# Hybrid SSD/GLA trunk, output stage: the norm's row scaling issued later, another arithmetic for the last two row pairs, and the last product in two halves

## The chip, the core and the metric

One NeuronCore of a Trainium2 chip runs the whole program as one launch. The metric is the device time of that launch in microseconds (us); each kernel is run several times and the median counts. Engines are called as in the profile: PE is the matrix engine (PEld its weight load), DVE the vector engine, ACT the scalar engine, POOL the GpSimd engine, SP the engine that here only issues DMAs. Each engine works through its own queue in order; a DMA is issued by an engine's queue and then moves by itself, and an instruction or a DMA issue whose data or buffer is not ready holds up what is behind it in that queue.

## The reference, cut to what matters

The kernel computes one layer of a decoder trunk on 2048 tokens of width 1024, in float32. `u = rmsnorm(h)` goes through one input projection into two branches (a Mamba-2 SSD scan and a gated linear attention), both are projected, gated and added to `merged`, and the end of it is

```python
merged = jnp.sum(gates * branch_proj, axis=2)
h = hres + jnp.einsum('bld,de->ble', merged, w_out)
...
out = rmsnorm(h, final_norm_w)[:, N_META:]   # x * rsqrt(mean(x*x) + EPS) * w, row by row
```

The change touches only this last product with `w_out`, the residual sum and the final row norm.

## The kernel before, in words

The kernel first runs the input projections and the two scans over four blocks of 512 tokens, and then seven stages of 1024-wide products (gates and two branch projections for each half of the tokens, then the output stage). Only the output stage, the last of the seven, is touched.

**Products.** Every stage multiplies 2x2 blocks by seven products in place of eight (a Strassen-like scheme). A float32 operand is split into a rounded high part and the rest (`hl`), so one block product of 128 rows, depth 512 and 512 columns is four depth steps of three matmuls (`accum`, L187 to L191): 12 matmuls of 128x128 by 128x512. In the output stage a "pair" is two tiles of 128 rows (i = 0 and 1) by two column halves (t = 0 and 1); there are 8 pairs, worked in four groups of two, and within a group the products run in the order `PS = (1, 2, 6, 7, 5, 3, 4)`, each for both pairs of the group: 14 products in a group, 56 in the stage. In the last group products 4 and 3 change places (L1112 to L1118).

**Banks and snapshots.** For a pair, products 1, 6, 5 and 3 add up in one PSUM bank ("a", printed as `pj`), 7 and 4 in another ("b", `pt`), 2 in a third ("c", `pc`). After products 1, 6 and 5 ACT copies bank "a" into an SBUF tile `sn` (`snapshot`, L1007, its instruction is L1010), and the next product into bank "a" waits for that copy. A quarter of the output is complete after products 2, 5, 4 and 3 (`DONE`, L1013); each then is handed to the stage's `use`: products 2 and 5 complete the first, 3 and 4 the second quarter of a row tile. `total` (L1023, its DVE add is L1026) adds bank and snapshot.

**Output stage** (`out_stage`, L1068). `fetch` loads a quarter of the residual x into a tile `io` (L1074, issued by SP; 8 such buffers, so exactly one group's quarters). `use` (L1080) adds the product to it on DVE (L1084: `r = 0.5*x + r`), squares it on ACT with a row sum into `ssf` (L1090), and when both quarters of a row tile are there: two tiny DVE instructions make mean + EPS (L1092, L1093), POOL raises it to -0.5 (L1094), and DVE scales both quarters by that column and by the norm weights (L1097, two instructions). `store` (L1016) only notes the two quarters; `flush` (L1162) issues the notes as DMAs from the ACT queue (L1164) after the next product, and what is left at the end of the program goes out from SP (L1215).

**What sets the order.** `at(position, fn)` books work at a product's position, and the main loop (L1206 to L1215) traces product, flush, booked work. `prep_a` (L980) splits a left operand on ACT (L983) and DVE (L984) five products ahead; `load_a` and `sum_a` (L962, L971) load the next group's left operands into tiles `ar` and form their sums `as` on POOL (L974 to L977), nine products ahead. SP's queue is exactly in traced order (`manual_schedule`). For all other engines, PE among them, a list scheduler at build time orders the instructions by its own estimate of when each can start; traced order is a priority there. Waits between engines follow from the tiles.

## Time and profile before

| what | value |
|---|---|
| device time, median of 3 runs | 2293.7 us (2292.3 to 2297.49) |
| device time of the profiled execution | 2293.83 us |
| its span, first to last instruction | 2292.0 us |
| mean granted PE clock | 0.994 |
| PE busy | 2232.7 us, 97% of the span |
| DVE, ACT, POOL busy | 68%, 51%, 30% |
| output stage's share | its matmuls run from about 2120 us to 2280.6 us of the span |

In a timeline row the columns are the start and the duration in us, engine and line, operation, output<-inputs, shapes, count; in square brackets how long the engine had been idle before and what ended that. "q" behind an engine means its queue, for DMA issues. In a row of the windows view they are the stretch, its length, then for PE, PEld, DVE, ACT and POOL the busy us with the number of instructions, the granted PE clock, the busy share of the DMA engines and GB/s. In the waits view a row is: who waited, for whom, us in total, times, longest.

### The profile page before, as it was taken

The numbers are of one execution on the slowest core, as the hardware profiler recorded it, in microseconds if no ns is written. First come the engines' busy times: TensorE is split into PE (matmuls) and PEld (weight loads), VectorE is DVE, ScalarE is ACT, GpSimd is POOL, SyncE is SP. The second block draws the span as 40 slices with busy tenths as digits, with TensorE's granted clock in tenths as the row PEclk, the third lists the DMA queues.
The fourth block names the chain that finished last, engine by engine and source line by source line (L and its number), as shares of the span: only waits on it lengthen the run. The fifth ranks groups of instructions, "written<-read, shape, count | busy, mean of one in ns | idle before, by whom it ended". The sixth has DMA issues, their size and how long they took to land. (4 is left out here: it accounts for less than half of the span.)

```text
span 2292.0 us, 36448 instructions
## 1 busy us (share of the span) xinstructions
PE 2232.7 (97%) x12641; PEld 1944.7 (85%) x12641; DVE 1549.2 (68%) x2895; ACT 1180.1 (51%) x2726; POOL 683.8 (30%) x681
## 2 busy tenths in 40 slices
PE   7899999999999999999999999899999999999997
PEld 6899989888889988888888898778888888788776
DVE  5677676675666676667667666674678845788766
ACT  4665655465534455544455544454544545454443
POOL 3344433122222122211212100066333274323331
PEclk9999999999999999999999999999999999999999
DMA  8766776667787676877667654466768865787743
GB/s 298 234 208 216 272 258 211 219 205 231 245 270 218 221 225 208 264 256 245 206 220 223 219 185 157 130 216 211 234 224 292 300 226 197 245 278 262 244 145 121
DMA packets 301544, 518.04 MB, mean 226 GB/s; under 512 B 27696, under 2 KB 143664, under 8 KB 301360
## 3 DMA queue, kind: packets, MB, share of 16 engines
q1 hardware_dynamic: 200400, 402.84, 54.4%
q10 hardware_dynamic: 100960, 112.88, 14.2%
q8 instruction: 99, 1.62, 0.3%
q14 instruction: 85, 0.70, 0.1%
HBM read 368.42 MB, written 147.19 MB: 225 GB/s over the span
## 5 line engine op out<-in xcount | busy, mean ns | idle before, releaser
L189 PE MATMUL pj<-ue,whl 128*128 128x264 f32 (+1 forms) x672 | 238.8, 355 | 12.3 <-ACT acc L492 6.3
L191 PE MATMUL pj<-ue,whl 128*128 128x264 f32 (+1 forms) x672 | 232.3, 346 | 0.6 <-DVE tkc L399 0.6
L190 PE MATMUL pj<-ue,whl 128*128 128x264 f32 (+1 forms) x672 | 231.3, 344 | 0.0
L189 PE MATMUL pj<-uo,whl 128*128 128x512 f32 x512 | 206.6, 404 | 0.0
L191 PE MATMUL pj<-uo,whl 128*128 128x512 f32 x512 | 200.1, 391 | 0.0
L190 PE MATMUL pj<-uo,whl 128*128 128x512 f32 x512 | 199.4, 389 | 0.0
L82 POOL TENSOR_TENSOR wr<-wr 128x256 f32<-128x256 f32 x80 | 68.5, 857 | 430.6 <-DMA wr<-u 176.2
L189 PE MATMUL pj<-b,a 128*128 128x512 f32 x480 | 189.4, 396 | 6.6 <-ACT sn L1010 5.8
L191 PE MATMUL pj<-b,a 128*128 128x512 f32 x480 | 188.6, 393 | 0.0
L190 PE MATMUL pj<-b,a 128*128 128x512 f32 x480 | 187.8, 391 | 0.7 <-DVE b L959 0.7
L170 POOL TENSOR_TENSOR whl<-wr,whl 128x512 fp32r<-128x512 f32 (+1 forms) x100 | 134.0, 1347 | 181.0 <-ACT whl L169 132.8
L974 POOL TENSOR_TENSOR as<-ar,ar 128x512 f32<-128x512 f32 x40 | 59.1, 1476 | 396.3 <-DMA ar<-in_w_br 114.2
L496 DVE SCALAR_TENSOR_TENSOR acc<-cin,hcw,acc 128x512 f32<-128x512 f32 (+1 forms) x192 | 154.6, 805 | 28.8 <-ACT acc L492 27.9
L984 DVE TENSOR_TENSOR a<-ar,a 128x512 fp32r<-128x512 f32 x160 | 125.5, 793 | 57.0 <-ACT a L983 55.3
L959 DVE TENSOR_TENSOR b<-br,b 128x512 fp32r<-128x512 f32 x140 | 120.5, 877 | 52.6 <-ACT b L958 50.7
L189 PEld LDWEIGHTS pj<-ue,whl 128*128 128x128 f32 x672 | 128.9, 192 | 29.9 <-ACT acc L492 7.4
L189 PE MATMUL pj<-whl,ue 128*128 128x256 f32 (+1 forms) x496 | 144.1, 291 | 2.1 <-ACT ue L315 2.1
L189 PE MATMUL pj<-whl,uo 128*128 128x256 f32 (+1 forms) x496 | 143.3, 289 | 0.6 <-DMA whl<-k_zm 0.6
L191 PEld LDWEIGHTS pj<-ue,whl 128*128 128x128 f32 x672 | 128.9, 192 | 15.8 <-POOL whl L170 0.9
L191 PE MATMUL pj<-whl,ue 128*128 128x256 f32 (+1 forms) x496 | 140.6, 284 | 1.4 <-DVE ue L317 1.4
L190 PEld LDWEIGHTS pj<-ue,whl 128*128 128x128 f32 x672 | 129.1, 192 | 14.8
L191 PE MATMUL pj<-whl,uo 128*128 128x256 f32 (+1 forms) x496 | 140.8, 284 | 0.0
(308 smaller groups left out, 6535.2 us busy)
## 6 DMA issues: line engine op xcount, KB each, us to landing
whl<-k_s SPq DMA_DIRECT2D x96, 512.0 KB, 4.3
whl<-k_g SPq DMA_DIRECT2D x96, 512.0 KB, 4.2
whl<-k_v SPq DMA_DIRECT2D x48, 512.0 KB, 3.8
whl<-k_z SPq DMA_DIRECT2D x36, 512.0 KB, 3.7
wr<-in_w_feat SPq DMA_DIRECT2D x64, 256.0 KB, 4.4
k_s<-whl SPq DMA_DIRECT2D x32, 512.0 KB, 3.7
cb<-cumd ACTq DMA_DIRECT2D x64, 256.0 KB, 5.7
y<-gg ACTq DMA_DIRECT2D x64, 256.0 KB, 4.4
```

The source lines that it names most:

```text
L82: nc.gpsimd.tensor_tensor(o, x, y, op=ALU.subtract)
L170: nc.gpsimd.tensor_tensor(hl[:, 1], raw, hl[:, 0].bitcast(F32), op=ALU.subtract)
L189: nc.tensor.matmul(ps, sh, mh, start=first, stop=False, **kw)
L190: nc.tensor.matmul(ps, sh, ml, start=False, stop=False, **kw)
L191: nc.tensor.matmul(ps, sl, mh, start=False, stop=last, **kw)
L496: nc.vector.scalar_tensor_tensor(acc, cin[:, k:k + tt], hcw[:, ti, k:k + 1], acc, op0=ALU.mult, op1=ALU.add)
L959: nc.vector.tensor_tensor(t[:, 1], raw, t[:, 0].bitcast(F32), op=ALU.subtract)
L974: nc.gpsimd.tensor_tensor(s1, a21, a22, op=ALU.add)
L984: nc.vector.tensor_tensor(t[:, 1], src, t[:, 0].bitcast(F32), op=ALU.subtract)
```

## The change

1. **Row scaling later.** For the 12 row tiles whose last product is not among the last four of the stage, the mean and the power (`scale`) are traced one product after the row's last product, and the two scalings with their stores (`finish`) three products after it. `tc.issue_after` queues their DVE instructions behind the DVE instruction traced last (`latest`: an operand split or a residual add); it orders the queue and adds no wait.
2. **Last two pairs** (the last group): the snapshot is added to the residual first (`r += 0.5*snap`, SBUF only), then the bank (`r += 0.5*bank`), in place of bank into snapshot and the sum into r. As many DVE instructions as before; the bank is read by the second of them.
3. **PE order.** In the last 14 products PE too keeps traced order.
4. **The last product** is traced as two halves of 256 columns, 12 matmuls each, in one bank, each half with its own residual add and square. Its `ssf` tile has a third column.
5. **Last four rows' scaling** (`at_once`): not delayed. Three quarters that complete early in the last group are multiplied by the norm weights as soon as their squares are taken; in the last three rows ACT then scales the early quarter by the row factor (`AF.Identity` with a scale column) while DVE scales the late one. In the very last row the norm weights are multiplied in before the factor is known, the second half's multiplication queued behind the last mean instruction.

The diff, shortened:

```diff
@@ prep_a
-            nc.vector.tensor_tensor(t[:, 1], src, t[:, 0].bitcast(F32), op=ALU.subtract)
+            latest[:] = [nc.vector.tensor_tensor(t[:, 1], src, t[:, 0].bitcast(F32), op=ALU.subtract)]
@@ product
+            if (self, n, p) == order[-1]:
+                for c in (slice(0, HB), slice(HB, BLK)):
+                    for j in range(4):
+                        bt = self.b[p, j]
+                        accum(ps[:, c], (a[:, 0, j], a[:, 1, j]), (bt[:, 0, c], bt[:, 1, c]), False, j == 3,
+                              skip_group_check=True)
+                    self.use(n, *DONE[p], ps, None, c)
+                return
@@ out_stage
-        def use(n, i, t, ps, snap):
-            r0 = (2 * n + i) * P
+        def use(n, i, t, ps, snap, cols=None):
             r = res[n, i, t]
-            x = total(ps, snap)
-            nc.vector.scalar_tensor_tensor(r, x, 0.5, r, op0=ALU.mult, op1=ALU.add)
+            if snap is not None and n >= seq // (2 * P) - 2:
+                nc.vector.scalar_tensor_tensor(r, snap, 0.5, r, op0=ALU.mult, op1=ALU.add)
+            else:
+                ps = total(ps, snap)
             first = (n, i) not in ssq
             if first:
-                ssq[n, i] = mk(spl, [P, 2], F32, "ssf")
+                ssq[n, i] = mk(spl, [P, 3], F32, "ssf", bufs=8)
             q = ssq[n, i]
             jk = mk(spl, [P, BLK], BF16, "junk", bufs=1)
-            nc.scalar.activation(jk, r, AF.Square, accum_out=q[:, t:t + 1])
-            if not first:
-                nc.vector.tensor_tensor(q[:, 0:1], q[:, 0:1], q[:, 1:2], op=ALU.add)
-                nc.vector.tensor_scalar(q[:, 0:1], q[:, 0:1], 1.0 / D, EPS, op0=ALU.mult, op1=ALU.add)
-                nc.gpsimd.tensor_tensor(q[:, 0:1], q[:, 0:1], mhalf[:, 0:1], op=ALU.pow)
-                for hf in range(2):
-                    o = res[n, i, hf]
-                    nc.vector.scalar_tensor_tensor(o, o, q[:, 0:1], fns[hf], op0=ALU.mult, op1=ALU.mult)
-                    store(out[r0:r0 + P, hf * BLK:(hf + 1) * BLK], o)
+            c = cols or slice(0, BLK)
+            k = t + (c.start > 0)
+            latest[:] = [nc.vector.scalar_tensor_tensor(r[:, c], ps[:, c], 0.5, r[:, c], op0=ALU.mult, op1=ALU.add)]
+            nc.scalar.activation(jk[:, c], r[:, c], AF.Square, accum_out=q[:, k:k + 1])
+            row = n, i, t
+            if row == at_once[-1] or (first and (n, i) in [w[:2] for w in at_once[1:]]):
+                if k < 2:
+                    nc.vector.tensor_tensor(r[:, c], r[:, c], fns[t][:, c], op=ALU.mult)
+                if k == 1 and not first:
+                    mean(q)
+                if k == 2:
+                    last = nc.vector.scalar_tensor_tensor(q[:, 0:1], q[:, 2:3], 1.0 / D, q[:, 0:1],
+                                                          op0=ALU.mult, op1=ALU.add)
+                    nc.gpsimd.tensor_tensor(q[:, 0:1], q[:, 0:1], mhalf[:, 0:1], op=ALU.pow)
+                    with tc.issue_after(last.ins):
+                        nc.vector.tensor_tensor(r[:, c], r[:, c], fns[t][:, c], op=ALU.mult)
+                    finish(*row)
+            elif row in at_once:
+                scale(*row)
+                finish(*row)
...
+        def finish(n, i, t):
...
+            if (n, i, t) in at_once[1:]:
+                nc.scalar.activation(early, early, AF.Identity, scale=q)
+                if (n, i, t) == at_once[-1]:
+                    nc.vector.tensor_scalar(late, late, q, None, op0=ALU.mult)
+                else:
+                    nc.vector.scalar_tensor_tensor(late, late, q, fns[t], op0=ALU.mult, op1=ALU.mult)
+            else:
+                for o, fn in ((early, fns[1 - t]), (late, fns[t])):
+                    nc.vector.scalar_tensor_tensor(o, o, q, fn, op0=ALU.mult, op1=ALU.mult)
+            for hf, o in ((1 - t, early), (t, late)):
+                store(out[r0:r0 + P, hf * BLK:(hf + 1) * BLK], o)
+
+        def behind(fn, *row):
+            with tc.issue_after(latest[0].ins):
+                fn(*row)
+
+        for i, (n, p) in enumerate(out_order):
+            row = n, *DONE.get(p, (0, 0))
+            if p in (3, 4) and i + 4 < len(out_order):
+                later.append((i + 1, lambda row=row: behind(scale, *row)))
+                later.append((i + 3, lambda row=row: behind(finish, *row)))
+            elif p in (3, 4):
+                at_once.append(row)
@@ main loop
+        if i == len(order) - 2 * len(PS):
+            run_out.close()
+            run_out.enter_context(tc.manual_schedule(engines={mybir.EngineType.PE, mybir.EngineType.SP}))
```

`scale` is `mean` and the POOL power, `mean` the two tiny DVE instructions.

More of the change, by code (lines that the diff above doesn't have):

```diff
@@ L1011, in snapshot @@
             self.snap[n, p] = sn
+    latest, later, order = [], [], []
     DONE = {2: (0, 0), 5: (1, 1), 4: (1, 0), 3: (0, 1)}
@@ new lines, in mean, with scale @@
+        def mean(q):
+            nc.vector.tensor_tensor(q[:, 0:1], q[:, 0:1], q[:, 1:2], op=ALU.add)
+            nc.vector.tensor_scalar(q[:, 0:1], q[:, 0:1], 1.0 / D, EPS, op0=ALU.mult, op1=ALU.add)
+        def scale(n, i, t):
+            q = ssq[n, i]
+            mean(q)
+            nc.gpsimd.tensor_tensor(q[:, 0:1], q[:, 0:1], mhalf[:, 0:1], op=ALU.pow)
+        def finish(n, i, t):
+            r0 = (2 * n + i) * P
+            q = ssq[n, i][:, 0:1]
+            early, late = res[n, i, 1 - t], res[n, i, t]
+            if (n, i, t) in at_once[1:]:
[9 more added lines that the diff above has]
+                store(out[r0:r0 + P, hf * BLK:(hf + 1) * BLK], o)
@@ L1102, in out_stage, with pairs_of @@
                      fetch, use)
+    PS = (1, 2, 6, 7, 5, 3, 4)
+    def pairs_of(npairs, last=False):
+        return [(n + i, p) for n in range(0, npairs, 2)
+                for p in (PS[:5] + (4, 3) if last and n == npairs - 2 else PS) for i in range(2)]
+    out_order = pairs_of(seq // (2 * P), True)
     stages = []
@@ L1204, in trunk_kernel @@
         st.snapshot(n, 6)
[L1206 to L1215 removed]
+    run_out = ExitStack()
+    run_out.enter_context(tc.manual_schedule(engines={mybir.EngineType.SP}))
+    run(-1)
+    for i, (st, n, p) in enumerate(order):
+        if i == len(order) - 2 * len(PS):
+            run_out.close()
+            run_out.enter_context(tc.manual_schedule(engines={mybir.EngineType.PE, mybir.EngineType.SP}))
+        if i >= NEARLY:
+            due, stores[:] = stores[:], []
+            st.product(n, p)
+            flush(due)
+        run(i)
+    for dst, src in stores:
+        nc.sync.dma_start(dst, src)
+    run_out.close()
 def _layout(inputs):
```

21 lines of the change are left out of this document (5 added, 16 removed).

## The prediction

> **What bounds the kernel now.** I read the page's first part, then the windows of the output stage, then PE's timeline there for holes, then each hole backwards through the waits and timelines of ACT, DVE and POOL, and last the timelines behind the final matmul.
>
> ```profile
> span 2292.0 us, 36448 instructions
> PE 2232.7 (97%) x12641; PEld 1944.7 (85%) x12641; DVE 1549.2 (68%) x2895; ACT 1180.1 (51%) x2726; POOL 683.8 (30%) x681
> ...
> 2160.00:2180.00 20.00, 17.62 (x71) 13.90 (x70) 15.67 (x27) 7.23 (x15) 6.98 (x7) 0.91 0.66 221
> 2272.14 0.39 PE L189 MATMUL pt<-b,a 128*128 128x512 f32 x1
> 2274.89 0.39 PE L189 MATMUL pj<-b,a 128*128 128x512 f32 x1
> ```
>
> PE is the bound: 97% busy, and nothing in this change takes a matmul away. So time can come only from two places: holes in PE's stream inside the output stage, and what follows the last matmul. The last two rows give the pace: one product of 12 matmuls takes 2274.89 - 2272.14 = 2.75 us, 0.229 us for each start. The window 2160 to 2180 has PE busy 17.62 of 20 us and the clock at 0.91: there is a hole in it. PE's timeline shows three holes:
>
> ```profile
> 2172.19 0.39 PE L191 MATMUL pj<-b,a 128*128 128x512 f32 x1
> 2174.96 0.80 PE L189 MATMUL pj<-b,a 128*128 128x512 f32 x1 [2.38 <-ACT sn L1010]
> ...
> 2178.10 0.40 PE L190 MATMUL pj<-b,a 128*128 128x512 f32 x1
> ...
> 2214.89 0.39 PE L191 MATMUL pj<-b,a 128*128 128x512 f32 x1
> 2216.37 0.50 PE L189 MATMUL pj<-b,a 128*128 128x512 f32 x1 [1.09 <-ACT sn L1010]
> 2216.71 0.39 PE L190 MATMUL pj<-b,a 128*128 128x512 f32 x1
> ...
> 2224.51 0.40 PE L191 MATMUL pt<-b,a 128*128 128x512 f32 x1
> 2225.20 0.50 PE L189 MATMUL pj<-b,a 128*128 128x512 f32 x1 [0.29 <-ACT sn L1010]
> 2225.54 0.39 PE L190 MATMUL pj<-b,a 128*128 128x512 f32 x1
> ```
>
> From 2172.19 to 2178.10 lie eight starts; at 0.229 they take 1.83, they took 5.91: 4.08 us lost. In the second hole two starts took 1.82 in place of 0.46: 1.36. In the third 1.03 in place of 0.46: 0.57. Together **6.0 us**. All three wait for a snapshot (L1010) on ACT. Why is the snapshot late?
>
> ```profile
> 2170.30 1.30 POOL L974 TENSOR_TENSOR as<-ar,ar 128x512 f32<-128x512 f32 x1 [5.00 <-DMA ar<-m]
> 2171.55 0.55 POOL L1094 TENSOR_TENSOR ssf<-ssf,mhalf 128x1 f32<-128x1 f32 x1
> ...
> 2172.14 3.42 DVE L1097 SCALAR_TENSOR_TENSOR io<-io,ssf,br 128x512 f32<-128x512 f32 x2 [2.86 <-POOL ssf L1094]
> ...
> 2173.92 0.34 ACTq L1164 DMA_DIRECT2D out_h<-io  x1
> 2174.31 0.60 ACT L1010 ACTIVATE sn<-pj 128x512 f32<-128x512 f32 x1 [4.82 <-DVE io L1097]
> ...
> DVE io L1097 <- POOL ssf L1094: 14.8, 14, 5.2
> ACT sn L1010 <- DVE io L1097: 13.4, 3, 7.1
> ```
>
> Read it from the top. The power of a row (L1094) stands on POOL behind an operand sum (L974), which waits for its load. DVE stands at the row scaling (L1097) until that power is there; ACT's queue stands at the store of the scaled row; the snapshot stands behind the store; PE stands for the snapshot. The last two rows, from the waits view between 2130 us and the end, say that the pattern is general: 14.8 us of DVE on the power, 13.4 us of the snapshot on the scaling. The last PE row of each hole shows that the same chain ran in the next group of pairs.
>
> Behind the last matmul:
>
> ```profile
> 2280.16 0.40 PE L191 MATMUL pj<-b,a 128*128 128x512 f32 x1
> ...
> 2280.59 0.69 DVE L1084 SCALAR_TENSOR_TENSOR io<-pj,io 128x512 f32<-128x512 f32 x1
> ...
> 2283.48 0.63 ACT L1090 ACTIVATE junk<-io 128x512 bf16<-128x512 f32 x1
> 2284.01 0.19 ACT L1090 ACTIVATION_READ_ACCUMULATOR junk<-io 128x1 f32 x1
> ...
> 2285.16 0.15 DVE L1092 TENSOR_TENSOR ssf<-ssf 128x1 f32<-128x1 f32 x1
> ...
> 2286.55 0.15 DVE L1093 TENSOR_SCALAR ssf<-ssf 128x1 f32<-128x1 f32 x1
> 2286.85 0.55 POOL L1094 TENSOR_TENSOR ssf<-ssf,mhalf 128x1 f32<-128x1 f32 x1 [1.86 <-DVE ssf L1093]
> 2287.43 1.41 DVE L1097 SCALAR_TENSOR_TENSOR io<-io,ssf,br 128x512 f32<-128x512 f32 x2 [0.73 <-POOL ssf L1094]
> ...
> L1215 SPq DMA_DIRECT2D out_h<-io x2: 343/343/343, 2288.2 to 2288.9; - x2
> ```
>
> PE ends at 2280.56, the program at 2292.0: a tail of 11.44 us. The last product's residual add ends at 2281.28, the last square starts only at 2283.48; the mean's two instructions come at 2285.16 and 2286.55, between the scalings of other rows; the second of the last two stores is issued at 2288.9, and from there 3.1 us are fixed.
>
> **The change, part by part.**
>
> *Scaling three products later.* Per row it moves two DVE instructions (0.15 each), one power (0.55 undisturbed), two scalings (1.41) and two ACT store issues (0.34 each); nothing is added. The mean now comes one product, the scaling three products (8.25 us) after the row's last product in traced order, so the power has 5.5 us to appear before DVE reaches the scaling; the longest wait on it was 5.2. The stores follow their scalings in ACT's queue by one more product, so ACT meets a store whose data are written. I take all three holes as gone: **-6.0**. Bounds: 0 (the chain re-forms elsewhere), -6.0. If the cover is gone, what is late next is the residual load (rivals).
>
> The first hole contains a lower clock:
>
> ```profile
> 2174.96:2178.38 3.42, 3.42 (x9) 2.71 (x10) 2.94 (x7) 1.09 (x2) 1.00 (x2) 0.54 0.51 177
> ```
>
> After 2.38 us of idle PE ran 3.42 us at a granted clock of 0.54; after 1.09 us it did not. The Trainium skill, "TensorE: Matmul & The Clock Gate", Part 1, puts the fall to half clock behind an idle window of about 3.4 us, counted by a free-running window. By that figure a hole of this length would cost only its 2.54 us, and the sum below would be 1.5 us smaller; this trace shows the fall after less, and the measurement decides.
>
> *Residual into the snapshot.* Two 512-wide DVE instructions as before; one lies ahead of the product's end instead of behind it where DVE is free. In the last group products 5 and 4 share bank "b", and the bank's release moves from the first to the second instruction: product 4 may start 0.7 us later at worst, twice, if DVE is late. I take 0, since DVE is idle there:
>
> ```profile
> 2270.25 0.69 DVE L1026 TENSOR_TENSOR sn<-sn,pt 128x512 f32<-128x512 f32 x1 [1.36 <-ACT sn L1010]
> ```
>
> *Traced PE order* adds no matmul. Product 4 now ends before 3 for both pairs, so the rows of product 4 are finished earlier. Taken at 0.
>
> *Last product in two halves.* 24 matmuls of 256 columns for 12 of 512:
>
> ```profile
> 703.04 0.28 PE L189 MATMUL pj<-whl,uo 128*128 128x256 f32 x1
> 703.40 0.28 PE L189 MATMUL pj<-whl,uo 128*128 128x256 f32 x1
> L482 DVE SCALAR_TENSOR_TENSOR tok<-tok,pj 128x256 f32<-128x256 f32 x12 | 5.1, 422 | 15.6 <-ACT tok L481 15.6
> L596 ACT ACTIVATE junk<-tok 128x256 bf16<-128x256 f32 x64 | 26.4, 412 | 42.2 <-DVE tok L594 28.5 <-POOL wr L82 9.2 <-DVE act L500 3.6
> L618 ACT ACTIVATE gg<-pt,hsw 128x512 f32<-128x512 f32 x32 | 20.2, 685 | 0.0
> ```
>
> Three starts take 0.36 us, 0.12 each: 24 x 0.12 - 2.75 = **+0.13**. Both halves lie in one bank, and the first is read by DVE while PE would write the second. The trace shows no bank that is read between matmuls into it; every read, like the one at 2280.59, follows the bank's last matmul. So PE's wait for that read is bounded by 0 and by 0.03 + 0.42 (a 256-wide add with one operand from a bank, L482) + 0.1 for the signal, or 1.3 if a scaling of 0.7 stands ahead on DVE. I take **+0.55**, nearest to the rows. The Trainium skill, "PSUM — Partial Sum Buffer", "PSUM bank collisions raise a hardware error", says that two engines must not be in one bank and partitions at a time, even in different columns: by it the wait is certain; without it the sum would be 0.55 larger. No run here shows it.
>
> *The new tail,* from the last matmul's end: residual add of the second half 0.03 + 0.42; ACT's start 0.1 later (an estimate between POOL's 0.15 behind DVE, at 2286.70, and DVE's 0.03 behind POOL, at 2287.40); square and accumulator read 0.72 for 512 columns (2283.48 to 2284.20), less 0.63 - 0.41 = 0.50; mean 0.03 + 0.15; power 0.15 + 0.55; ACT scaling of the early quarter 0.03 + 0.69 (L618, a scale column and 512 columns); first store issue 0.03 later, second about 0.43 behind it (0.34 each, with a gap of 0.1, an estimate); 3.1 to the end. Sum 6.2. DVE's own scaling of the late quarter lies beside ACT's and needs no more than the 0.7 of an L1097. So 11.44 - 6.2 = **-5.2**. Bounds: another row's scaling of 0.7 ahead of the residual add, and its two store issues, 0.9, ahead of ACT's scaling.
>
> **Sum:** -6.0 + 0.13 + 0.55 - 5.2 = -10.5. The profiled execution took 2293.83 us (its span and 1.8 around it): 2283.3. It stands 0.1 above the median of 2293.7, so I forecast **2283.2 us**. With the bounds of tail and bank, its own range is 2281.5 to 2286. About 0.2% (4.6 us) is what a measurement of this kernel can tell from no change.
>
> **Rivals.**
>
> *The holes stay, the tail goes.* The scheduler may still put a power behind a sum on POOL, or the scaling may meet some other late operand. For it: DVE and POOL are ordered by an estimate, not by the source; two of the holes came from an order which the source did not ask for. Against it: 5.5 us more room. Time: 2293.7 - 4.5 = 2289.2.
>
> *The tail stays, the holes go.* Scalings of rows not yet finished, or the stores of the row before on ACT, stand ahead of the last row's steps, as now. 2293.7 - 6.0 + 0.7 = 2288.4.
>
> *Slower: residual loads come too late.* There are 8 `io` buffers, and SP's queue waits for stores already:
>
> ```profile
> SPq L1074 <- DMA out_h<-io: 55.7, 14, 11.4
> DVE io L1084 <- DMA io<-in_xm: 7.5, 3, 3.5
> 2159.64 1.41 DVE L1097 SCALAR_TENSOR_TENSOR io<-io,ssf,br 128x512 f32<-128x512 f32 x2 [0.67 <-POOL ssf L1094]
> ```
>
> SP stands up to 11.4 us for a store, with the operand loads of a later group behind it. A store 8.25 us later delays the first residual of the next group, DVE's residual add (three such waits already), the splits behind it on DVE, the squares and snapshots on ACT, and then PE, at each of the three group changes. It decides from a slip above the 8.25 us between a snapshot and the product that needs it three products later. If half of the slip came through at each change, with 1.5 us each for the clock (4.08 less the bare 2.54), it costs 3 x (4.1 + 1.5) = 17: 2300. Against it: the first row of a group is scaled at 2159.64 now, although its product ends near 2150 (11 products of 2.75 from 2120), so it is late already; in the new order it comes behind the adds of the group's last product, which ends near 2158.5 (14 products), and a split, near 2161 to 2162. The true slip is then 2 to 3 us, not 8.
>
> *The change doesn't do what it says:* the order inside DVE could leave the scalings where they are, which is the first rival's time.
>
> **How the numbers follow.** Forecast 0.68; holes stay 0.15; tail stays 0.08; slower 0.09. The range reaches from 2281 to 2289.5, leaving out the slow rival and the upper part of the first. Faster by over 0.2% means below 2289.1: the forecast, most of the second rival, half of the first: 0.82. Same: 0.09. Slower: 0.09. The likeliest time is 2283.2.
>
> **What would show it.** The waits of L1097 on the power near 0, and no PE start of the last 160 us with more than 0.5 us to the one before, except a hole of 0.5 to 1.3 in the middle of the last product. The last matmul ends near 2275.2 (2280.56 - 6.0 + 0.7). The tail is 6.2 long, its last store issued 3.1 before the end. I am wrong if the tail exceeds 8 us, if DVE's waits for residual loads grow beyond 15 us, or if a snapshot still ends PE's idle time.

## The result

| | before | after |
|---|---|---|
| device time, median of 4 runs each | 2294.95 us (2292.3 to 2297.49) | 2282.97 us (2279.31 to 2285.52) |
| ratio after/before | | **0.9948**, 95% interval 0.9932 to 0.9965 |
| profiled execution, its span | 2293.83, 2292.0 us | 2279.31, 2277.5 us |
| output stage: start of its first matmul into "pc" to the end of the last matmul | 155.29 us | 149.80 us |
| tail: from there to the end of the span | 11.49 us | 6.78 us |

The change makes the kernel 0.5% faster; 2283.2 us was forecast. The two spans differ by 14.5 us, but the stage and its tail only by 166.78 - 156.58 = **10.2 us**. The other 4.3 us lie ahead of the output stage, where every engine's instructions and every queue's DMA issues come in the same order in both traces. In the eleven runs below the stage's first matmul came at 2122.3 to 2125.6, at 2125.27 in the profile before and at 2120.93 here: the profiled execution of the changed kernel happened to be early. So all comparisons below are of the stage's matmuls and the tail, not of spans.

**The profile after.** Lines have moved: the power is L1128 (was L1094), the scaling L1142 (L1097), the residual add from the bank L1102 (L1084), the snapshot L1018 (L1010). First the page, then the windows view for the stage and for the window shown of before:

```profile
span 2277.5 us, 36482 instructions
PE 2227.8 (98%) x12653; PEld 1944.2 (85%) x12653; DVE 1548.0 (68%) x2899; ACT 1182.4 (52%) x2731; POOL 681.9 (30%) x681
```

```profile
2120.93:2270.73 149.80, 149.28 (x661) 122.24 (x659) 111.53 (x186) 70.61 (x151) 46.15 (x39) 1.00 0.53 171
2160.00:2180.00 20.00, 20.00 (x89) 16.35 (x88) 14.69 (x24) 8.92 (x20) 7.36 (x6) 1.00 0.70 228
```

PE is busy 149.28 of the stage's 149.80 us; between 2160 and 2180 it was busy 17.62 us at a clock of 0.91 before, and is busy all 20 at full clock now. What is left is one hole of 0.52. It is in the middle of the last product (PE's timeline):

```profile
2268.25 0.28 PE L191 MATMUL pj<-b,a 128*128 128x256 f32 x1
2269.05 0.39 PE L189 MATMUL pj<-b,a 128*128 128x256 f32 x1 [0.52 <-DVE io L1102]
```

The first half's last matmul ends at 2268.53; the residual add reads the bank for 0.42; only then does the second half start. The waits that carried the argument, from 2120 us on, and SP's own:

```profile
DVE io L1102 <- DMA io<-in_xm: 4.0, 2, 3.4
...
DVE io L1142 <- POOL ssf L1128: 1.6, 3, 0.7
...
ACT sn L1018 <- DVE io L1142: 1.1, 1, 1.1
```

```profile
SPq L1083 <- DMA out_h<-io: 54.2, 12, 14.9
```

DVE waited 14.8 us for the power before and 1.6 now; the snapshot 13.4 us for the scaling and 1.1 now; DVE's wait for residual loads went from 7.5 to 4.0 at the same add (and 0.8 at the new one, L1092), and SP's wait for stores at the residual loads from 55.7 to 54.2.

The place where PE stood empty for 2.4 us before, early in the second group, now (the timelines of POOL and DVE):

```profile
2165.53 0.55 POOL L1128 TENSOR_TENSOR ssf<-ssf,mhalf 128x1 f32<-128x1 f32 x1 [2.27 <-DVE ssf L1123]
2166.12 1.42 DVE L1142 SCALAR_TENSOR_TENSOR io<-io,ssf,br 128x512 f32<-128x512 f32 x2
...
2167.45 0.69 DVE L1102 SCALAR_TENSOR_TENSOR io<-sn,io 128x512 f32<-128x512 f32 x1
...
2169.51 1.29 POOL L974 TENSOR_TENSOR as<-ar,ar 128x512 f32<-128x512 f32 x1 [3.43 <-DMA ar<-m]
...
2171.27 1.78 DVE L1102 SCALAR_TENSOR_TENSOR io<-sn,io 128x512 f32<-128x512 f32 x1
```

The first group's fourth power runs 4 us ahead of the next operand sum on POOL (L974), and the last two scalings end by 2167.54, before that sum. Keep the two residual adds in mind: the same instruction takes 0.69 at 2167.45 and 1.78 at 2171.27, where POOL is summing.

The tail, ACT, DVE, POOL and SP together:

```profile
2270.77 0.42 DVE L1102 SCALAR_TENSOR_TENSOR io<-pj,io 128x256 f32<-128x256 f32 x1 [0.26 <-PE pj L191]
2270.91 0.72 ACT L1135 ACTIVATE io<-io,ssf 128x512 f32<-128x512 f32 x1 [1.19 <-POOL ssf L1128]
...
2271.54 0.40 ACT L1103 ACTIVATE junk<-io 128x256 bf16<-128x256 f32 x1
...
2272.07 0.16 DVE L1111 SCALAR_TENSOR_TENSOR ssf<-ssf 128x1 f32<-128x1 f32 x1 [0.21 <-ACT junk L1103]
...
2272.31 0.66 POOL L1113 TENSOR_TENSOR ssf<-ssf,mhalf 128x1 f32<-128x1 f32 x1 [1.43 <-DVE ssf L1111]
2273.00 0.72 ACT L1135 ACTIVATE io<-io,ssf 128x512 f32<-128x512 f32 x1 [0.97 <-POOL ssf L1113]
...
2273.75 0.82 SPq L1284 DMA_DIRECT2D out_h<-io  x2
```

Every step of the forecast is there in its order: add, square, mean, power, ACT's scaling, two stores. One step is late: the square could start at 2271.2 and starts at 2271.54, behind the scaling of the row before (2270.91) in ACT's queue.

### The profile page after: what moved, and what is told of

The parts are those of the page before. It is cut to its first block, busy times and chain, and to the rows that moved or that the text cites. A ratio compares the mean times of both kernels' runs of the same rounds, so it can differ in the third digit from the quotient of the medians.

```text
span 2277.5 us, 36482 instructions
## 1 busy us (share of the span) xinstructions
PE 2227.8 (98%) x12653; PEld 1944.2 (85%) x12653; DVE 1548.0 (68%) x2899; ACT 1182.4 (52%) x2731; POOL 681.9 (30%) x681
## 4 chain that ended last, share of the span: by engine, by line
PE 81%; DMA 5%; DVE 5%; ACT 4%; issue 3%; POOL 2%; SPq 0%; ACTq 0%; POOLq 0%; DVEq 0%
PE pj L189 19%; PE pj L191 18%; PE pj L190 18%; PE pt L189 3%; PE pt L190 3%; PE pt L191 3%; PE pc L581 2%; PE pc L189 2%; PE pc L191 2%; PE pc L190 2%; PE pc L732 2%; PE pc L582 1%; PE pc L584 1%; DMA acc<-in_xmt 1%; PE pc L840 1%
## 5 line engine op out<-in xcount | busy, mean ns | idle before, releaser
L189 PE MATMUL pj<-b,a 128*128 128x512 f32 (+1 forms) x484 | 188.9, 391 | 2.3 <-ACT sn L1018 1.7
L190 PE MATMUL pj<-b,a 128*128 128x512 f32 (+1 forms) x484 | 187.9, 388 | 1.0 <-DVE b L959 0.9
L191 PE MATMUL pj<-b,a 128*128 128x512 f32 (+1 forms) x484 | 188.8, 390 | 0.0
L974 POOL TENSOR_TENSOR as<-ar,ar 128x512 f32<-128x512 f32 x40 | 57.0, 1424 | 382.8 <-DMA ar<-in_w_br 145.0
```

The costliest lines, as they stand in the source:

```text
L189: nc.tensor.matmul(ps, sh, mh, start=first, stop=False, **kw)
L190: nc.tensor.matmul(ps, sh, ml, start=False, stop=False, **kw)
L191: nc.tensor.matmul(ps, sl, mh, start=False, stop=last, **kw)
L974: nc.gpsimd.tensor_tensor(s1, a21, a22, op=ALU.add)
```

## The experiments

Eleven kernels ran. "Matmuls" is the stage from its first matmul into "pc" to the end of the last matmul, "tail" what follows, both from the one profiled execution; time is the median, and the ratio is against runs of the kernel before on the same chip. Runs 5 to 8 ran on one chip and the other seven on another, so across the two the ratios are to be compared.

| run | time, us | ratio, 95% interval | matmuls | tail | sum |
|---|---|---|---|---|---|
| before | 2293.3 to 2294.95 | 1 | 155.29 | 11.49 | 166.78 |
| after | 2282.97 | 0.9948 [0.9932, 0.9965] | 149.80 | 6.78 | 156.58 |
| 1 scaling later, alone | 2286.59 | 0.9973 [0.9964, 0.9982] | 148.93 | 11.33 | 160.26 |
| 2 parts 2 to 5, alone | 2290.7 | 0.9986 [0.9975, 0.9996] | 155.95 | 6.80 | 162.75 |
| 3 before, POOL in traced order | 2290.25 | 0.9983 [0.9973, 0.9992] | 153.85 | 11.48 | 165.32 |
| 4 scaling nine products later | 2289.78 | 0.9979 [0.9969, 0.999] | 156.72 | 6.95 | 163.67 |
| 5 scaling one product later | 2283.59 | 0.9955 [0.9939, 0.997] | 150.74 | 6.79 | 157.54 |
| 6 no rule for DVE's queue | 2284.22 | 0.9955 [0.9941, 0.997] | 151.13 | 6.79 | 157.93 |
| 7 last product whole | 2283.46 | 0.9954 [0.9938, 0.9971] | 148.93 | 7.69 | 156.63 |
| 8 own bank, tail reordered | 2281.76 | 0.9947 [0.9935, 0.996] | 149.01 | 7.11 | 156.12 |
| 9 as 5, POOL in traced order | 2283.72 | 0.9958 [0.9944, 0.9973] | 151.15 | 6.80 | 157.95 |
| 10 as 1, nine products later | 2286.93 | 0.9974 [0.9962, 0.9986] | 149.45 | 11.88 | 161.32 |
| 11 as 8, DVE's tail reordered | 2282.7 | 0.9955 [0.9942, 0.9967] | 149.14 | 6.80 | 155.94 |

The theory at the start was the prediction's: part 1 removes the holes because the power no longer stands behind an operand sum, and parts 2 to 5 shorten the tail. The rivals: one part does both; the holes depend on POOL's order alone, not on the later scaling; a still later scaling turns slower through late residual loads.

### Runs 1 and 2: the parts by themselves

Run 1 is the kernel before with the mean and the power one and the scalings three products later:

```diff
-            if not first:
-                ... mean, power, two scalings and stores at once
+                later.append((i + 1, lambda row=row: behind(scale, *row)))
+                later.append((i + 3, lambda row=row: behind(finish, *row)))
```

> The kernel before with part 1 alone: mean and power one product later, scaling three products later for the 12 rows; the last group, the last product and the last four rows stay as they were. If the holes come from the row scaling standing in DVE's and ACT's queues (my theory), all three holes go: from the output stage's first matmul on bank c to the last matmul 6.0 to 6.4 us less, the tail stays at 11.5; ratio to before about 0.9973. If the holes needed something of the last-group parts, or if the delayed stores hold up the residual loads (rival), less than 3 us go or it gets slower.

Run 2 is the changed kernel with mean, power and scalings back at the row's last product:

```diff
-                later.append((i + 1, lambda row=row: behind(scale, *row)))
-                later.append((i + 3, lambda row=row: behind(finish, *row)))
+                now.append(row)
...
-            elif row in at_once:
+            elif row in at_once or row in now:
```

> The changed kernel without part 1: every row scaled at once again, with the new arithmetic, order, halves and tail in the last group. My theory: the three holes of about 6 us in the groups before stay, the last product keeps its hole of 0.8, the tail is 6.8 as in the changed kernel; 11.5 - 6.8 - 0.9 = 3.8 us faster than before, ratio about 0.9983. Rival (the parts need each other, as rows not yet finished stand ahead of the last row's steps): the tail stays above 9 us.

Run 1 shortens the matmuls by 6.36 and leaves the tail (-0.16); no start in the stage comes late. Run 2 has the holes again, each with the same releaser, and the tail of the changed kernel. Sums: -6.52 and -4.03, together -10.55 against -10.2 for the change. **The two gains are separate and add up.** Run 2's first hole shows the clock's fall too (PE's timeline, then the windows view):

```profile
2173.54 0.77 PE L189 MATMUL pj<-b,a 128*128 128x512 f32 x1 [2.25 <-ACT sn L1018]
```

```profile
2173.54:2176.96 3.42, 3.42 (x8) 2.75 (x9) 2.94 (x7) 1.10 (x2) 1.00 (x2) 0.51 0.53 184
```

### Run 3: the power's place alone

The kernel before, with GpSimd's queue in the order of the source throughout the output stage, so that a group's four powers precede the operand sums traced behind them; nothing is scaled later.

```diff
+        if i == begins[-1]:
+            run_out.close()
+            run_out.enter_context(tc.manual_schedule(engines={mybir.EngineType.Pool, mybir.EngineType.SP}))
```

> The kernel before, with one thing changed: in the output stage POOL too keeps traced order, so that the powers stand ahead of the next group's operand sums, nothing is delayed. If a power behind a sum is the whole cause, the first two holes go, the third with them, 5 to 6 us. If the room of three products is what counts (rival), DVE still waits 0.5 to 0.7 us on each power and the stores still hold the snapshots: at least 2 us of holes stay.

The waits for the power shrank; of the 6.36 us of holes only 1.44 came back, and not evenly. A group is counted here from its first matmul into "pc" to the next group's; without a hole it takes 38.58 us, the last one 33.19. The kernel before takes 38.83, 42.71, 40.55 and 33.19, run 3 takes 40.01, 42.06, 38.58 and 33.19. So the third group lost its holes: there the power's place was enough. The first group's 1.43 us come from something else: its hole ends ahead of the stage's first scaling, and its snapshot stands on ACT behind the split of a right operand (L958) whose load came late (ACT's and PE's timelines):

```profile
2142.55 0.63 ACT L958 ACTIVATE b<-br 128x512 fp32r<-128x512 f32 x1 [2.13 <-DMA br<-out_t]
2143.09 0.58 ACT L1010 ACTIVATE sn<-pj 128x512 f32<-128x512 f32 x1
...
2143.72 0.50 PE L189 MATMUL pj<-b,a 128*128 128x512 f32 x1 [1.16 <-ACT sn L1010]
```

In the second group 3.48 of 4.13 us stayed, most of it in a gap of 3.02 from start to start. The timelines of POOL, DVE, ACT and PE around it, then the waits on the power:

```profile
2172.28 1.29 POOL L974 TENSOR_TENSOR as<-ar,ar 128x512 f32<-128x512 f32 x1
2172.35 3.48 DVE L1097 SCALAR_TENSOR_TENSOR io<-io,ssf,br 128x512 f32<-128x512 f32 x2 [0.66 <-POOL ssf L1094]
...
2175.75 1.79 DVE L984 TENSOR_TENSOR a<-ar,a 128x512 fp32r<-128x512 f32 x1
...
2180.01 0.40 PE L191 MATMUL pt<-b,a 128*128 128x512 f32 x1
...
2182.39 0.58 ACT L1010 ACTIVATE sn<-pj 128x512 f32<-128x512 f32 x1
...
2183.03 0.50 PE L189 MATMUL pj<-b,a 128*128 128x512 f32 x1 [2.62 <-ACT sn L1010]
```

```profile
DVE io L1097 <- POOL ssf L1094: 8.1, 14, 0.8
```

The longest wait for a power is 0.8 in place of 5.2. But now the two scalings run beside the sums and take 3.48 in place of 1.41, the split behind them 1.79 in place of 0.69; the residual adds, the squares and the snapshot come behind that. **So the theory that the power's place is all falls in the second group.** A scaling at a group's end can lose in two ways: it waits for a power that is queued behind the sums, or it runs beside the sums at less than half its speed.

### Runs 5, 6 and 9: what the three products buy

Run 5 scales one product later, run 6 drops the rule that keeps a scaling behind the newest residual add or split, run 9 is run 5 with POOL in traced order.

```diff
-                later.append((i + 3, lambda row=row: behind(finish, *row)))
+                later.append((i + 1, lambda row=row: behind(finish, *row)))
```

> The kernel after with the scalings one product behind the row's last product in place of three (the mean and the power stay one behind; everything else as changed). Theory 'room': what empties PE before the change is that two scalings, their stores and the power stand ahead of the next snapshot's operands on DVE and ACT at a group's end; with one product of room DVE waits for the power again (about 0.5 to 0.8 us for each row, some 8 us in the stage against 1.6) and part of the holes comes back: the stage's matmuls last 150.5 to 153, time 2284 to 2287. Rival 'the power's place on POOL is all': four powers ahead of the next group's sums are enough, no hole but the one in the last product, matmuls 149.8, time 2283.0. In both the tail stays near 6.8.

```diff
         def behind(fn, *row):
-            with tc.issue_after(latest[0].ins):
-                fn(*row)
+            fn(*row)
```

> The kernel after without the rule that holds a mean and a scaling back until the newest residual add or split on DVE has been issued; they are still called one and three products later. Theory 'the room does it': no hole at a group's end, matmuls of the stage 149.8 within 0.3, time 2283.0 within 0.1%. Rival 'the rule does it': the scalings slip ahead of adds and splits again, at least one hole of over 1 us with a snapshot at its end comes back, matmuls above 151, time above 2284.5. The tail stays near 6.8 in both.

```diff
+        if i == begins[-1]:
+            run_out.close()
+            run_out.enter_context(tc.manual_schedule(engines={mybir.EngineType.Pool, mybir.EngineType.SP}))
...
-            run_out.enter_context(tc.manual_schedule(engines={mybir.EngineType.PE, mybir.EngineType.SP}))
+            run_out.enter_context(tc.manual_schedule(engines={mybir.EngineType.PE, mybir.EngineType.Pool, mybir.EngineType.SP}))
```

> The kernel with the scalings one product behind the row (as in the run above that asked for the room), with GpSimd in traced order throughout the output stage, so that every power stands ahead of the next group's operand sums. Theory 'the power's place is what the room buys': with the powers ahead of the sums one product of room is enough, no hole at a group's end, matmuls of the stage 149.8 within 0.3, waits of the scalings on the power at most 1 us each. Rival 'the room itself': the scalings still lie beside the sums on DVE's slow time and hold the adds back, a hole of 1 us or more with a snapshot at its end stays, matmuls 150.8 or more.

In runs 5 and 6 one hole is back, with a snapshot at its end: starts 1.06 and 1.29 apart in the second group, matmuls +0.94 and +1.33. In both, POOL put the last two powers of the first and of the second group behind three operand sums, and the scalings wait 11.7 us for powers, 4.3 at the longest. No scaling is slow: the longest of L1142's 26 takes 754 ns in either run. So here the wait alone makes the hole. Run 6 has the three products of room and still this order: the rule in `behind` decides where the power lands on POOL as much as the distance does. By the matmuls the theory "room" fits run 5 (150.5 to 153 expected) and the rival fits run 6 (above 151); the times, 2283.59 and 2284.22, lie a little below those expected with them and within the scatter of the changed kernel's (2279.31 to 2285.52). But run 5 doesn't tell room from the power's place, since the powers moved behind the sums with it. Run 9 does.

Run 9 takes the waits away (0.7 at the longest) and keeps the hole. Its waits on the power, then the timelines of DVE, POOL and PE:

```profile
DVE io L1142 <- POOL ssf L1128: 5.3, 10, 0.7
```

```profile
2171.33 1.40 POOL L974 TENSOR_TENSOR as<-ar,ar 128x512 f32<-128x512 f32 x1
2171.51 3.47 DVE L1142 SCALAR_TENSOR_TENSOR io<-io,ssf,br 128x512 f32<-128x512 f32 x2
...
2174.39 1.75 POOL L976 TENSOR_TENSOR ar<-ar,ar 128x512 f32<-128x512 f32 x1
2174.90 0.67 DVE L1035 TENSOR_TENSOR sn<-sn,pc 128x512 f32<-128x512 f32 x1
2175.50 1.19 DVE L984 TENSOR_TENSOR a<-as,a 128x512 fp32r<-128x512 f32 x1
...
2180.34 0.51 PE L189 MATMUL pj<-b,a 128*128 128x512 f32 x1 [0.93 <-ACT sn L1018]
```

Here too the rival holds: two scalings fall into the sums' time and take 3.47, and a hole comes back without a long wait. One row of each trace says which kernels do that (the source view of the scaling's line: shortest, middle and longest duration in ns), first before, then run 9, then the changed kernel:

```profile
L1097 DVE SCALAR_TENSOR_TENSOR io<-io,ssf,br x32: 743/750/1770, 2159.6 to 2288.1; 128x512 f32<-128x512 f32 x32
```

```profile
L1142 DVE SCALAR_TENSOR_TENSOR io<-io,ssf,br x26: 742/750/1790, 2159.0 to 2269.3; 128x512 f32<-128x512 f32 x26
```

```profile
L1142 DVE SCALAR_TENSOR_TENSOR io<-io,ssf,br x26: 744/749/754, 2157.6 to 2264.9; 128x512 f32<-128x512 f32 x26
```

In the changed kernel none of the 26 scalings is slowed by a sum. That is what its order buys, beside the power's place.

### Runs 4 and 10: the slower rival

Run 4 is the changed kernel with the scalings nine products later, run 10 is run 1 with the same.

```diff
-                later.append((i + 3, lambda row=row: behind(finish, *row)))
+                later.append((i + 9, lambda row=row: behind(finish, *row)))
```

> The changed kernel with the scaling nine products after the row's last product in place of three: the stores come 16.5 us later again. The slow rival of the prediction made strong: SP waits for stores by 16.5 us more at each of three group changes, DVE's residual adds of product 2 wait for their loads. By the slack of 8.25 us between a snapshot and the product that needs it, about 8 us of PE time is lost at each change and the clock falls: 25 to 30 us slower than the changed kernel. If residual buffers do not matter: no change.

> The kernel before with its scalings nine products later and nothing else (the residual is added behind the product's end everywhere, as before). The run with nine products and the new last group had a hole of 4.23 us in its last group, where an accumulator waited for the add of a residual that came late. Theory 'that hole is part two's, the bank's release hangs on the residual': here the bank is released by the snapshot's add alone, so residuals come just as late (SP waits for stores over 80 us in sum) but PE has no hole anywhere: matmuls of the stage 149.0 within 0.4. Rival 'a late residual holds PE through DVE's queue in any case' (the prediction's slower rival): a hole of 3 us or more in the last group, matmuls above 152.

In run 4 the loss of 25 to 30 us that was expected at the three group changes did not come: the first three groups take 38.84, 38.58 and 38.58 us against 38.58, although SP waits 84.7 us for stores. The last group has a hole (SP's waits, DVE's and PE's timelines, the windows view):

```profile
SPq L1083 <- DMA out_h<-io: 84.7, 14, 24.7
```

```profile
2263.40 0.40 PE L191 MATMUL pj<-b,a 128*128 128x512 f32 x1
...
2266.28 0.69 DVE L1092 SCALAR_TENSOR_TENSOR io<-sn,io 128x512 f32<-128x512 f32 x1 [0.98 <-DMA io<-in_xm]
2266.89 0.68 DVE L1102 SCALAR_TENSOR_TENSOR io<-pt,io 128x512 f32<-128x512 f32 x1
...
2267.62 0.79 PE L189 MATMUL pt<-b,a 128*128 128x512 f32 x1 [3.83 <-DVE io L1102]
```

```profile
2267.62:2272.90 5.28, 5.28 (x12) 4.12 (x13) 3.04 (x5) 1.45 (x4) 0.00 (x0) 0.50 0.33 99
```

In the last two pairs the snapshot goes into the residual (L1092) and only then the bank (L1102). So the bank's release hangs on a residual load; elsewhere the bank is added to the snapshot, which needs no load. Here the load is late, PE stands 3.83 us, and the next 12 matmuls run at a clock of 0.50. The last group takes 40.72 us in place of 34.06.

Run 10 tells the two apart. Its loads are as late (SP waits 84.9 us; DVE waits six times and 8.6 us for residuals), its banks do not hang on them, and its last group takes 33.19 us with no hole. The matmuls take 149.45, 0.05 over the range expected; the surplus lies in the first group (39.09 in place of 38.58). Run 10 also lacks part 3, and PE runs one product 3 ahead of product 4 there. That is not the reason: in run 10 bank "b" is free for the first product 4 at 2261.25, 21.1 us after the last group's start (2240.17), and in run 4 that product was due 22.0 us after it. **In these runs a late residual load reaches PE only through part 2's bank.**

### Runs 7, 8 and 11: the halves and the tail

Run 7 leaves the last product whole:

```diff
-                for c in (slice(0, HB), slice(HB, BLK)):
+                for c in (slice(0, BLK),):
```

> The kernel after with its last product undivided: 12 matmuls of 512 columns, one residual add, one square. PE gains the hole between the halves and the longer weight loads: last matmul about 0.9 us earlier against the stage's start. The tail loses the parallel work: the add takes 0.69 in place of 0.42, the square with its read 0.72 in place of about 0.5, and the product with the norm's weight comes behind the add: tail 7.2 to 7.6 in place of 6.8. By the prediction's terms (+0.13 and +0.55 against 0.5 of shorter chain) the sum is -0.4 to 0 of 2283: the halves are worth nothing. Rival 'halving pays': the tail grows by more than 1.0 and the time with it by over 0.2.

The matmuls gain 0.87, the tail loses 0.91, and the sum differs by 0.05. **The halves show no worth here.** The tail is a little longer than expected because the last power takes 0.93 beside a 512-wide product with the norm's weight, in place of 0.66 beside the 256-wide one.

Run 8 puts the second half into a bank of its own, queues the scaling of the row before behind the last square on ACT, and issues one of the last four stores on ACT's queue:

```diff
-                for c in (slice(0, HB), slice(HB, BLK)):
+                own = bank(pc, "pc")
+                for c, bk in ((slice(0, HB), ps), (slice(HB, BLK), own)):
...
+                    with tc.issue_after(square.ins):
+                        finish(*at_once[2])
...
-        nc.sync.dma_start(dst, src)
+        q.dma_start(dst, src)
```

> The kernel after with three edits at its end: the second half of the last product accumulates in a bank of its own (the snapshot's half is added to the residual early on DVE), so that no read of the first half stands between; the scaling of the last-but-one row comes behind the last square on ACT instead of ahead of it; of the last four stores one is issued on ACT's queue. Theory (the hole of 0.80 between the halves is the bank's, and the 0.35 by which the last square is late is ACT's scaling of the other row): the hole goes to below 0.1, the last square starts within 0.1 of its add's end, stage 156.6 less 0.7 less 0.35 less up to 0.4 for the stores = 155.2, time about 2281.6, a ratio of 0.9942 to before. Rival 'the hole is the weight load's or the order's, not the bank's': the hole stays at 0.8 and the stage at 156.2. Rival 'the delayed row becomes the end': its stores land last and the tail stays at 6.8.

The bank's part came out as said: the second half starts 0.12 behind the first, the hole is gone, matmuls -0.79. The square starts 0.09 behind its add. But the tail is 7.11, not 6.0. Two DVE instructions moved into the chain (timeline):

```profile
2272.60 0.43 DVE L1112 TENSOR_TENSOR io<-io,br 128x256 f32<-128x256 f32 x1
...
2273.07 0.42 DVE L1107 SCALAR_TENSOR_TENSOR io<-pc,io 128x256 f32<-128x256 f32 x1
...
2273.82 0.75 DVE L1147 SCALAR_TENSOR_TENSOR io<-io,ssf,br 128x512 f32<-128x512 f32 x1 [0.27 <-POOL ssf L1136]
...
2274.49 0.15 DVE L1116 SCALAR_TENSOR_TENSOR ssf<-ssf 128x1 f32<-128x1 f32 x1
```

The last add starts 0.30 behind the last matmul's end (2272.77), because the first half's product with the norm's weight stands ahead; the last mean starts 0.40 behind the end of the square's read (2274.09), because the other row's scaling stands ahead of it on DVE. Run 11 moves both behind:

```diff
-                if k < 2:
+                if first:
                     nc.vector.tensor_tensor(r[:, c], r[:, c], fns[t][:, c], op=ALU.mult)
...
+                    with tc.issue_after(latest[0].ins):
+                        nc.vector.tensor_tensor(r[:, :HB], r[:, :HB], fns[t][:, :HB], op=ALU.mult)
...
+                    finish(*at_once[2], square.ins, norm.ins)
```

> The run with the own bank once more, with two instructions of DVE moved: the scaling of the last-but-one row stands behind the last mean and the last product with the norm's weight (it had stood ahead of that mean, waiting 0.27 for its power and taking 0.75), and the first half's product with the norm's weight stands behind the last residual add (it had kept that add 0.30 back). Theory (the tail of 7.11 there is the 6.78 of the kernel after, less 0.35 for the square, plus these two): tail 6.4 to 6.5, stage 155.4, time about 2281.1. Rival 'the stores' landing sets the tail, not DVE's order': the tail stays above 6.9.

DVE's order did what was expected: from the last matmul's end to the issue of the last store it is 2276.63 - 2273.85 = 2.78 us, against 2274.18 - 2270.73 = 3.45 in the changed kernel. But the four last stores are now issued within 1.1 us (2275.55 to 2276.63) and land later (source view of the final stores: shortest, middle and longest us to landing; the changed kernel, then run 11):

```profile
DMA to landing us min/median/max: 2.0/2.2/2.3
```

```profile
DMA to landing us min/median/max: 2.1/2.5/3.0
```

From the issue of the last store to the end it is 4.02 us, against 3.34. That takes back all of the 0.67 that DVE's order gave, and the tail is 6.80: between theory (6.4 to 6.5) and rival (over 6.9), both partly right. Runs 8 and 11 have the smallest sums (156.12 and 155.94 against 156.58), yet their times, 0.9947 [0.9935, 0.996] and 0.9955 [0.9942, 0.9967], cannot be told from the changed kernel's. No version is shown to be faster than the changed one.

## Why the prediction was right, step by step

- **PE is the bound, and time comes from holes and tail alone.** Right: 10.2 us, 5.5 from the matmuls and 4.7 from the tail.
- **Holes gone, -6.0.** Right in size: run 1 gave -6.36, the three holes and a small one of 0.25 at 2144 us, which lies ahead of the first scaling and so can't be the change's doing. The reason given was only half. The prediction blamed the power behind the sum, and said that 5.5 us of room cure it. Its own rows had the other half: 3.42 us for two scalings (L1097) at 2172.14, and 1.41 for two at 2287.43. The two scalings ran beside POOL's sums at less than half speed, which adds 2.0 us to the wait of 2.86. Runs 3 and 9 removed the long waits and kept a hole in the second group; runs 5 and 6 had no slow scaling and a hole from the wait. The three products and the rule for DVE's queue work because, in this order, the powers and the scalings both end before the sums begin.
- **Halves +0.13, bank wait +0.55.** Together 0.68; measured 0.87, the last group's 34.06 (34.05 in run 2) against 33.19 (run 1). The idle time itself is 0.52, the prediction's 0.03 + 0.42 + 0.1 to within 0.03; from start to start the hole adds 0.68 (0.80 in place of 0.12), and the start behind it 0.10 (0.22 in place of 0.12), which was not forecast. The prediction said that the trace shows no bank that is read between matmuls into it. That was misread: the three holes are such cases, PE waiting for the snapshot's read of bank "a", and PE starts 0.05 behind the read's end (2174.31 + 0.60, then 2174.96), which would have been a row for its 0.1. The Trainium skill, "PSUM — Partial Sum Buffer", "PSUM bank collisions raise a hardware error", says that two engines must not be in one bank and the same partitions at a time, even at different addresses. The trace agrees as far as it goes: it shows the wait that the program makes, and run 8 that another bank removes it. What the chip does without the wait was not tried.
- **Tail 6.2.** Measured 6.78, the mis-sized term. The add, square, mean, scaling and the two issues have the durations forecast. What was missed: the square's start, 0.35 behind its add's end in place of 0.1, since ACT was scaling the row before; the power, 0.66 in place of 0.55; and 3.34 from the last issue to the end in place of 3.1. The bound "another row's scaling ahead" was named, and priced at DVE and not at ACT, where it fell.
- **Residual into the snapshot, traced order: 0.** Right as the kernel stands. Run 4 shows the price when the residual is late: 6.7 us.
- **Sum -10.5, 2283.2 us.** Measured in the stage: -6.36 + 0.87 - 4.71 = -10.2. The terms missed by -0.4, +0.2 and +0.5, which partly cancel. That the median, 2282.97, lies 0.2 from the forecast is luck: the four runs reach from 2279.31 to 2285.52, and against the kernel before measured with them the median fell by 12.0.
- **Rivals.** "The holes stay" is run 2's case by another road, 2290.7 against 2289.2 said. "The tail stays" is run 1, 2286.59 against 2288.4 said. "Residual loads too late" was wrong in place: at the group changes late loads do not reach PE even at nine products (runs 4 and 10). The slip was small, as said: the first scaling comes 36.7 us after the first matmul into "pc" (2157.6 - 2120.9) in place of 34.4 (2159.64 - 2125.27), 2.3 us of the 2 to 3, and SP's waits at the residual loads did not grow (54.2 against 55.7). The mechanism that does turn slower needs two things that the prediction had on separate lines: a late residual and a bank whose release needs it.
- **What would show it.** Waits for the power 1.6; one hole, 0.80 from start to start; the last matmul 4.5 us earlier than said only by the early execution (2270.73 + 4.34 = 2275.07 against 2275.2); tail under 8; residual waits under 15. All as listed.

## What to carry to other kernels

Before a wait is blamed, read the duration of what follows it: a row that takes twice its usual time is a second cause, and curing the wait alone leaves it (runs 3 and 9). An instruction that frees a bank should not need anything that comes by DMA late; where it does, two harmless delays add up to one on the bound engine (runs 4 and 10). In a tail of a few microseconds every move puts something else into the chain: splitting the last product paid back about what it cost (0.91 for 0.87), and the last stores' landing took what DVE's order gave.

## What the runs showed of the hardware

- **DVE beside POOL.** Scalings (both tiles in SBUF) take 0.74 to 0.75 alone and 1.75 to 1.79 beside POOL's 512-wide sums; residual adds from a snapshot 0.69 and up to 1.8; the sum of a snapshot and a bank (L1026 before, L1035 in run 9) takes 0.67 to 0.69 in every run even there, as at 2174.90 in run 9. The Trainium skill, "SBUF — State Buffer", "Who interferes with whom", says that a DVE instruction with two SBUF inputs contends with a GpSimd instruction that reads SBUF, and one with at most one such input, outside its 2-port modes, does not. The traces agree in these rows; no run took the sums away by themselves. The prediction should have weighed it, since it bears on every two-input instruction of this stage.
- **The clock.** Idle times of 2.38 (before), 2.25 (run 2) and 3.83 us (run 4) were followed by 3.42, 3.42 and 5.28 us at 0.54, 0.51 and 0.50. In run 3 an idle time of 2.62 us was followed by full clock, so its length alone does not decide. The granted clock changes in steps of 3.41 us: the stretches at half clock last 3.41 us (before, from 2174.66), 3.41 (run 2, from 2173.61) and 6.83, twice as long (run 4, from 2266.14). In the kernel before the next fall comes 109.23 us later, at 2283.89, 32 steps of 3.413. In run 3 it falls behind the last matmul, at 2280.66, which puts a step's edge at 2181.67, in the middle of the idle time. The windows view, cut along these steps, around the first hole of the kernel before, then for the two steps of run 3 that share the idle time:

```profile
2171.25:2174.66 3.41, 1.33 (x6) 0.75 (x4) 2.52 (x2) 0.35 (x1) 3.41 (x4) 1.00 0.48 156
2174.66:2178.07 3.41, 3.11 (x7) 2.48 (x8) 2.93 (x6) 1.39 (x3) 1.30 (x2) 0.50 0.49 177
```

```profile
2178.26:2181.67 3.41, 2.15 (x10) 1.42 (x8) 3.39 (x5) 0.72 (x2) 1.62 (x1) 1.00 0.26 77
2181.67:2185.08 3.41, 2.06 (x9) 1.72 (x10) 1.24 (x2) 3.31 (x8) 0.00 (x0) 1.00 0.00 0
```

  The clock fell behind a step in which PE was busy 1.33 us (before), 1.17 (run 2) or 1.06 (run 4), and did not fall behind one with 2.15 or 2.06. Counted over all 13 traces from 300 us on, each along its own steps, PE was busy 1.70 us or less in the 26 steps ahead of a fall, and 1.65 or more in the 7489 other steps at full clock. So in these traces the clock falls when PE is busy for less than about half of such a step; an idle time that lies across two steps can be spared, and one of 2.25 us within a step is enough. The Trainium skill, "TensorE: Matmul & The Clock Gate", Part 1, has the free-running window of about 3.4 us, and the steps agree with it; but it speaks of an idle window, and here a window with PE busy up to half of the time was enough.
- **Stores close together.** Four stores of 128x512 issued within 1.1 us landed in 2.1 to 3.0 us (run 11), four within 1.4 in 2.1 to 2.6 (run 8), two 0.4 apart in 2.0 to 2.3 (after). In runs 8 and 11 one of the four went out on ACT's queue; no run parts that from their closeness.
